# Attention's values in two products a key tile instead of three, with the weight sums taken by adding DMAs

## The chip, the cores and the metric

The kernel runs on one core of a Trainium2 chip. The metric is the device time of one execution in microseconds: the median over runs, 3317.97 us before the change (3 runs, 3317.39 to 3322.92 us). A difference under 0.2%, some 6.6 us, is about what such a measurement cannot tell from none.

## The reference

One layer of a bidirectional hybrid encoder on 2048 + 256 tokens of width 1024, all in float32: an RMS norm and one input projection, eight mLSTM heads (forward and backward) beside eight attention heads of dimension 64 (two key/value heads, q and k normed and rotated), an output projection, then a gated MLP with a width-3 convolution. The part that the change touches is the attention:

```python
s = jnp.einsum('bqhgd,bkhd->bhgqk', qi, k).astype(jnp.float32) * scale
p = jax.nn.softmax(s, axis=-1)
return jnp.einsum('bhgqk,bkhd->bqhgd', p.astype(v.dtype), v)
```

Each row of the softmax needs both the product of the exponentials with the values and the sum of the exponentials over all keys.

## The kernel before

The kernel has four stages on one timeline. Phase A (to about 220 us) norms and projects all tokens to q, k, v and the gates and stores them in DRAM. Then attention and mLSTM run mixed: two generators, `attention` and `mlstm`, are stepped in turn by `run_both` so that both finish at a set ratio, and when mLSTM is done, `phase_c` (the output projection, tile `po`, L1001) is stepped beside the rest of attention. Phase D (the MLP, from about 1760 us) ends the kernel. The calls only emit instructions; a scheduler of the framework then sets each engine's order by its own simulated clock and by priorities, and each engine runs its own list strictly in that order.

Float32 matrix products are made of rounded parts: a number is split in a high part (rounded to the type `F32R`, which TensorE takes in one pass) and a low part, the rest. A product of two such numbers is high x high + high x low + low x high.

Attention works on 36 half blocks (`hbs`): 512 query columns of one head (or of two heads for the 256 short tokens) against all their keys. 32 have 16 key tiles of 128, taken two at a time as 8 key pairs (`kp`); four have one key pair. That is 260 key pairs. For each:

- `scores` (L576 to L590): four products of 512 columns into the two-bank PSUM tile `ps` (L583, L584), ScalarE's exponential into `pe` (L587), ScalarE's rounding of it into the high part of `xx` (L588), VectorE's difference into the low part (L589). `pe` has PEB = 2 buffers, `xx` XB = 4.
- `values` (L592 to L602), which follows PLAG = 3 key pairs later: for each of the two key tiles three products of 512 columns into the accumulator `pv` (one bank, 128 rows). The weights tile `vv` holds the high part of v in its columns 0 to 63 and ones in columns 64 to 127, so rows 64 to 127 of `pv` collect the sums of the weights. `vl` holds the low part of v. The products are `vv` with high `xx` (L600), `vl` with high `xx` (L601), `vv` with low `xx` (L602).
- `maxstep` (L545): for the next half block, two products (`px`, L560) and one VectorE maximum (L562), so that the maxima are known before its first exponential.

When the last key pair's values are done, `fin1` (L604) copies the values to `o1` and the sums to `rs` with four ScalarE copies (L612); one key pair later `fin2` (L614) takes reciprocals, multiplies, and stores to `mix_d` (L624). PSUM tiles of `scores`, `maxstep`, `prep` and `prep2` share one ring of two, tag `sc`.

GpSimd's list in this stage holds mLSTM's small steps: loads of `dm` and their triangular masks (L824, L828), the products `kw` (L793), the square roots `mr` (L97, L98), memsets, and the stores of attention's outputs (L624). A DMA that GpSimd issues stands in the same list: GpSimd first waits for the DMA's operands and only then goes on.

Of the kernel before, what the change touches and what calls it, by code (L numbers as in the profile page):

```python
# [70 lines left out]
PB = 4  # L71
PEB = 2
XB = 4
PLAG = 3
ZT = 3
# [382 lines left out]
def attention(g, tc, s1, s2, pp):  # L458
# [12 lines left out]
    def load_kv(grp, k0, k1, after=None):  # L471
# [6 lines left out]
        for t0 in range(0, n, 4):  # L478
            m = min(4, n - t0)
            s = f"{n}_{t0}"  # L480
            kk = sp.tile([P, m * P], F32R, tag="kk" + s, name=f"kk{grp}_{s}", bufs=1)
            kl1 = sp.tile([65, m * P], F32R, tag="kl1" + s, name=f"kl1{grp}_{s}", bufs=1)
            vv = sp.tile([P, m, P], F32R, tag="vv" + s, name=f"vv{grp}_{s}", bufs=1)
            vl = sp.tile([P, m, HD], F32R, tag="vl" + s, name=f"vl{grp}_{s}", bufs=1)
            c = slice((k0 + t0) * P, (k0 + t0 + m) * P)
            if after is not None:
                for t in (kk[0:1, 0:1], kk[HD:HD + 1, 0:1], kl1[0:1, 0:1], vv[0:1, 0, 0:1], vl[0:1, 0, 0:1]):
                    nc.gpsimd.tensor_copy(t, after[0:1, 0:1])
            nc.gpsimd.memset(f32(vv[:, :, HD:P]), 1.0)
            for r in (0, HD):  # L490
                nc.gpsimd.dma_start(f32(kk[r:r + HD, :]), g.k_d[grp, 0:HD, c])
            nc.gpsimd.dma_start(f32(kl1[0:HD, :]), g.k_d[grp, HD:P, c])
            nc.gpsimd.memset(f32(kl1[64:65, :]), 1.0)
            for a, t in ((0, vv[:, :, 0:HD]), (1, vl)):
                nc.gpsimd.dma_start(f32(t), g.v_d[grp, :, k0 + t0:k0 + t0 + m, a])
            parts.append((kk, kl1, vv, vl))

# [79 lines left out]
    def scores(s, kp):  # L577
# [10 lines left out]
        nc.scalar.activation(x[:, 0], pe, AF.Copy)  # L588
        nc.vector.tensor_tensor(x[:, 1], pe, f32(x[:, 0]), ALU.subtract)  # L589
        return kp, x  # L590

    def values(s, kp, x):  # L592

        if kp == 0:
            s.pv = pp.tile([P, 512], F32, tag="pv", name="pv" + s.nm, bufs=1)
        vv, vl = s.kv[kp // 2][2:4]
        for z in range(2):
            kt = 2 * kp + z
            x1, x2 = (x[:, a, z * 512:(z + 1) * 512] for a in range(2))
            nc.tensor.matmul(s.pv, vv[:, kt % 4, :], x1, start=kt == 0, stop=False)  # L600
            nc.tensor.matmul(s.pv[0:HD], vl[:, kt % 4, :], x1, start=False, stop=False)  # L601
            nc.tensor.matmul(s.pv, vv[:, kt % 4, :], x2, start=False, stop=kt == s.nk - 1)  # L602

    def fin1(s):  # L604

        s.o1 = sp.tile([P, 256], F32, tag="o1", name="o1" + s.nm, bufs=1)
        if s.n == len(hbs) - 3:
            g.hold = s.o1
        s.rs = sp.tile([P, 256], F32, tag="rs", name="rs" + s.nm, bufs=1)
        for z in range(2):  # L610
            for r, o in ((0, s.o1), (HD, s.rs)):
                nc.scalar.activation(o[HD * z:HD * z + HD], s.pv[r:r + HD, 256 * z:256 * z + 256], AF.Copy)  # L612

    def fin2(s):  # L614
        for t in range(2):
# [23 lines left out]
    def drain():  # L639
        b, kp, x = pend.pop(0)  # L640
        values(b, kp, x)
        if kp == b.nk // 2 - 1:
            fin1(b)
            fins.append(b)

    for n in range(len(hbs)):
# [4 lines left out]
        for kp in range(nkp):  # L651
            pend.append((cur, *scores(cur, kp)))
            ready = bool(fins)
            if len(pend) > PLAG:
# [6 lines left out]
            if ready:  # L661
                fin2(fins.pop(0))
            yield 2.3
# [5 lines left out]
    while pend:  # L669
        drain()  # L670
        yield 1
    for b in fins:
        fin2(b)

# [777 lines left out]
def body(tc, aps, phases="abcd"):  # L1452
# [5 lines left out]
    with ExitStack() as st:  # L1458
# [35 lines left out]
        with ExitStack() as s2:  # L1494
# [26 lines left out]
            pm = pool(s_m, "m_p", bufs=MB, space=PSUM, side="right")  # L1521
            sk = pool(s2, "b_k", bufs=1)
            sa = pool(s2, "b_s", bufs=2)
            pa = pool(s2, "b_p", bufs=SCB, space=PSUM)
# [138 lines left out]
```

## Time and profile before

| what | value |
|---|---|
| median of the runs | 3317.97 us |
| span of the profiled execution | 3315.5 us (the runs' median is 2.5 us above it: what lies around the span) |
| TensorE (PE) busy | 3240.5 us, 98% |
| VectorE (DVE) busy | 2429.5 us, 73% |
| ScalarE (ACT) busy | 1993.5 us, 60% |
| GpSimd (POOL) busy | 522.1 us, 16% |
| bytes moved by DMA | 612.31 MB, 185 GB/s in the mean |
| first and last start of a score product (L583) | 219.7 and 1748.7 us |

Busy time of PE is a union of modelled intervals that overlap: a product of 512 columns is shown as some 400 ns long, but the next one starts before its end. What a product costs is read from the distance of two starts. A DMA row gives the kilobytes of one DMA and the median time from its issue to its landing.

### The profile page before, as it was taken

To read this page: it belongs to the slowest core of one execution; us is meant where nothing else is said; L and a number is where in the kernel's file an instruction comes from. 1 tells how busy PE (TensorE), PEld (TensorE's weight loads), DVE (VectorE), ACT (ScalarE), POOL (GpSimd) and SP (SyncE) were. 2 spreads that over 40 slices of the span, in tenths; PEclk is the share of its full clock that TensorE was granted. 3 is DMA by queue.
4 is the path that set the end of the run, shared out by engine and by line. 5 is a ranking of instruction groups with operands and counts; after the bars stand their busy time and mean duration, and the time that the engine had idled before them with its cause. 6 is when DMAs were issued, how large, how long until landed. Compare 5 with 4: busy or idle time off the path is not lost.

```text
span 3315.5 us, 53149 instructions
## 1 busy us (share of the span) xinstructions
PE 3240.5 (98%) x19488; PEld 3018.0 (91%) x19488; DVE 2429.5 (73%) x3759; ACT 1993.5 (60%) x3738; POOL 522.1 (16%) x917
## 2 busy tenths in 40 slices
PE   8989999999999999999999999999999999999998
PEld 7878888888888888788889999999999999999998
DVE  7755676676657768866666899998888889666654
ACT  5646666666675776655454555665676667454543
POOL 4561042223224323200000000000000000020101
PEclk9999999999999999999999999999999999999999
DMA  9973333343346444423227666767676567968663
GB/s 353 316 213 101 112 103 113 98 125 109 99 139 189 123 147 127 139 96 106 76 93 266 220 222 213 248 229 271 202 254 240 194 224 239 320 216 276 216 226 134
DMA packets 359117, 612.31 MB, mean 185 GB/s; under 512 B 31029, under 2 KB 215271, under 8 KB 358855
## 3 DMA queue, kind: packets, MB, share of 16 engines
q1 hardware_dynamic: 329431, 563.14, 50.5%
q0 software_dynamic: 11856, 33.96, 3.8%
q10 hardware_dynamic: 17568, 11.80, 1.1%
q8 instruction: 154, 2.52, 0.3%
q14 instruction: 108, 0.88, 0.1%
HBM read 444.85 MB, written 163.93 MB: 184 GB/s over the span
## 4 chain that ended last, share of the span: by engine, by line
PE 83%; issue 5%; DMA 4%; ACT 3%; DVE 3%; POOL 2%; SPq 1%; POOLq 0%; ACTq 0%; DVEq 0%
PE pa L1164 17%; PE pc L1164 8%; PE pf L1428 7%; PE po L1001 6%; PE pb L1164 4%; PE mj L720 4%; PE pj L238 4%; PE mv L730 4%; PE ph L1428 3%; PE ps L583 3%; PE pv L602 3%; PE pv L600 3%; PE ps L584 3%; PE pv L601 3%; PE px L560 3%
## 5 line engine op out<-in xcount | busy, mean ns | idle before, releaser
L589 DVE TENSOR_TENSOR xx<-pe,xx 128x1024 fp32r<-128x1024 f32 x260 | 319.0, 1227 | 171.4 <-ACT xx L588 169.9
L587 ACT ACTIVATE pe<-ps 128x1024 f32<-128x1024 f32 x260 | 266.1, 1024 | 231.8 <-PE ps L584 215.0
L562 DVE TENSOR_REDUCE mx<-px 128x1 f32<-128x1024 f32 x256 | 310.5, 1218 | 100.6 <-PE px L560 100.0
L588 ACT ACTIVATE xx<-pe 128x1024 fp32r<-128x1024 f32 x260 | 275.1, 1058 | 5.2 <-PE pv L602 0.2
L1381 POOL TENSOR_TENSOR sq<-sq,sq 128x384 f32<-128x384 f32 x38 | 48.5, 1277 | 1382.7 <-ACT sq L1377 1302.2
L1001 PEld LDWEIGHTS po<-cmx,wo 128*128 128x128 f32 x1728 | 229.9, 189 | 19.5 <-DVE cx L1008 1.1
L1001 PE MATMUL po<-cmx,wo 128*128 128x256 f32 x1728 | 238.7, 283 | 1.4 <-DVE cx L1008 1.0
L1168 ACT ACTIVATE u<-pa 128x386 f32<-128x386 f32 (+2 forms) x264 | 128.9, 489 | 173.9 <-PE pa L1164 168.7
L600 PE MATMUL pv<-xx,vv 128*128 128x512 f32 x520 | 212.4, 408 | 10.5 <-ACT rs L612 6.0
L583 PE MATMUL ps<-qq,kk 128*128 128x512 f32 x520 | 213.8, 411 | 8.2 <-ACT pe L587 3.9
L602 PE MATMUL pv<-xx,vv 128*128 128x512 f32 x520 | 211.0, 406 | 3.5 <-DVE xx L589 3.4
L584 PE MATMUL ps<-qm,kl 65*128 65x512 f32 x520 | 208.9, 402 | 0.0
L601 PE MATMUL pv<-xx,vl 128*64 128x512 f32 x520 | 207.3, 399 | 0.0
L720 PEld LDWEIGHTS mj<-mn,wm 128*128 128x128 f32 x1296 | 178.3, 193 | 18.3 <-ACT og L736 4.5
L720 PE MATMUL mj<-mn,wm 128*128 128x256 f32 x1296 | 189.6, 288 | 2.8 <-ACT og L736 2.8
L730 PE MATMUL mv<-wm,mn 128*128 128x256 f32 x1296 | 189.9, 286 | 1.3 <-ACT qb L726 1.3
L730 PEld LDWEIGHTS mv<-wm,mn 128*128 128x128 f32 x1296 | 176.1, 190 | 15.2 <-ACT qb L726 2.3
L238 PE MATMUL pj<-w_a,n1T 128*128 128x512 f32 (+1 forms) x864 | 167.8, 353 | 11.0 <-ACT w_a L105 7.1
L560 PE MATMUL px<-kk,qq 128*128 128x512 f32 x512 | 167.2, 408 | 2.4 <-ACT pe L587 2.4
L238 PEld LDWEIGHTS pj<-w_a,n1T 128*128 128x128 f32 x864 | 141.3, 192 | 30.6 <-ACT w_a L105 7.1
L1164 PE MATMUL pc<-nt,wb 128*128 128x386 f32 (+2 forms) x792 | 148.0, 341 | 0.0
L831 ACT ACTIVATE dm<-dm,tm 128x128 f32<-128x128 f32 x288 | 94.8, 392 | 86.0 <-POOL dm L828 85.7
(337 smaller groups left out, 8106.0 us busy)
## 6 DMA issues: line engine op xcount, KB each, us to landing
mn<-n_d SPq DMA_DIRECT2D x216, 256.0 KB, 3.1
ru<-w_up SPq DMA_DIRECT2D x88, 512.0 KB, 5.1
rs<-wsu_d SPq DMA_DIRECT2D x88, 512.0 KB, 5.7
act_d<-ts SPq DMA_DIRECT2D x33, 768.0 KB, 6.4
nt<-act_d SPq DMA_DIRECT2D x60, 384.0 KB, 5.2
re_t<-wsd_d SPq DMA_DIRECT2D x45, 512.0 KB, 5.4
wsu_d<-tw SPq DMA_DIRECT2D x44, 512.0 KB, 4.2
act_d<-ya SPq DMA_DIRECT2D x99, 192.0 KB, 2.1
```

Of the source, the lines that this page charges most:

```text
L238: nc.tensor.matmul(pjs[t][:, c0:c1], nTs[tiles[t]][:, c, a, :], ws[c][:, b, c0:c1], start=(c == 0 and k == 0), stop=(c == NCC - 1 and k == 2))
L562: nc.vector.tensor_reduce(s.mx[:, t0, z0:z0 + 1], ps, AX.X, ALU.max)
L583: nc.tensor.matmul(o, kk[:, kc:kc + P], s.qq, start=True, stop=False)
L584: nc.tensor.matmul(o, kl1[:, kc:kc + P], s.qm, start=False, stop=True)
L589: nc.vector.tensor_tensor(x[:, 1], pe, f32(x[:, 0]), ALU.subtract)
L600: nc.tensor.matmul(s.pv, vv[:, kt % 4, :], x1, start=kt == 0, stop=False)
L602: nc.tensor.matmul(s.pv, vv[:, kt % 4, :], x2, start=False, stop=kt == s.nk - 1)
L720: nc.tensor.matmul(pj[:, o].rearrange("p (n t) -> p n t", t=P), s.w[c][:, a, o * P:(o + 1) * P], nT[c][:, :, h, :], start=(c + o + k == 0) ...
L730: nc.tensor.matmul(pv[:, o], nT[c][:, o, a, :], s.w[c][:, h, 256:512], start=(c + o + k == 0), stop=(c == NCC - 1 and k == 2 and o == 1))
L1001: nc.tensor.matmul(po[:, o], wo[c][z // 2][:, a, n], mx[c][:, h, :], start=c + o + k == 0, stop=c == NCC - 1 and o == 1 and k == 2)
L1164: s.nc.tensor.matmul(p, w[:, aa, c, :], ops[k][:, c, bb, 0:s.n], start=c == 0 and i == 0 and not add, stop=c == NCC // 2 - 1 and i == 2, s ...
L1428: nc.tensor.matmul(ps[c], w[:, aa, c, :], t[:, gi - g0, bb, 0:H], start=gi == 0 and m == 0 and not more, stop=gi == NG - 1 and m == 2, ski ...
```

## The change

Each key tile gets two products instead of three: the weights tile `vv` now holds v's high part in columns 0 to 63 and its low part in columns 64 to 127, and the first product is that tile with the high part of `xx` (all 128 rows of `pv`), the second is v's high part alone with the low part of `xx` (rows 0 to 63). The ones are gone from the weights, so `pv` no longer holds the sums. Instead an adding DMA, issued by GpSimd, adds the previous key pair's `pe` (for the first, the pair before; a chain through the half block) into this key pair's `pe`, 128 x 1024 numbers in float32, 512 KB. After the last key pair GpSimd adds the two halves (`asum`), `fin2` splits it in high and low, and `fin3` multiplies both with a tile of ones on TensorE, which sums over the 128 partitions and spreads the result. `fin1` now adds the two halves of `pv`, and the old `fin2` is `fin4`. These four steps go out one key pair apart. PEB goes from 2 to 3, XB from 4 to 3, PLAG from 3 to 2.

```diff
-PEB = 2
-XB = 4
-PLAG = 3
+PEB = 3
+XB = 3
+PLAG = 2
...
         nc.vector.tensor_tensor(x[:, 1], pe, f32(x[:, 0]), ALU.subtract)
+        if kp:
+            nc.gpsimd.dma_start(pe, s.acc, accum_op=ALU.add)
+        s.acc = pe
+        if kp == s.nk // 2 - 1:
+            s.acc = sp.tile([P, 512], F32, tag="asum", name="asum" + s.nm, bufs=1)
+            nc.gpsimd.tensor_tensor(s.acc, pe[:, 0:512], pe[:, 512:1024], ALU.add)
...
-            nc.tensor.matmul(s.pv, vv[:, kt % 4, :], x1, start=kt == 0, stop=False)
-            nc.tensor.matmul(s.pv[0:HD], vl[:, kt % 4, :], x1, start=False, stop=False)
-            nc.tensor.matmul(s.pv, vv[:, kt % 4, :], x2, start=False, stop=kt == s.nk - 1)
+            for a in (0, 1) if z == 0 else (1, 0):
+                if a:
+                    nc.tensor.matmul(s.pv[0:HD], vv[:, kt % 4, 0], x2, start=False, stop=False)
+                else:
+                    nc.tensor.matmul(s.pv, vv[:, kt % 4].rearrange("p a d -> p (a d)"), x1, start=kt == 0,
+                                     stop=kt == s.nk - 1)
...
         for z in range(2):
-            for r, o in ((0, s.o1), (HD, s.rs)):
-                nc.scalar.activation(o[HD * z:HD * z + HD], s.pv[r:r + HD, 256 * z:256 * z + 256], AF.Copy)
+            r, c = slice(HD * z, HD * z + HD), slice(256 * z, 256 * z + 256)
+            nc.scalar.activation(o2[r], s.pv[HD:P, c], AF.Copy)
+            nc.vector.tensor_tensor(s.o1[r], s.pv[0:HD, c], o2[r], ALU.add)
+
+    def fin2(s):
+
+        s.ah = sp.tile([P, 2, 512], F32R, tag="ah", name="ah" + s.nm, bufs=1)
+        nc.scalar.activation(s.ah[:, 0], s.acc, AF.Copy)
+        nc.vector.tensor_tensor(s.ah[:, 1], s.acc, f32(s.ah[:, 0]), ALU.subtract)
+
+    def fin3(s):
+
+        ps = pp.tile([P, 1024], F32, tag="sc", name="pa" + s.nm)
+        for a in range(2):
+            nc.tensor.matmul(ps[:, 0:512], g.onesr, s.ah[:, a], start=a == 0, stop=a == 1)
+        s.rs = sp.tile([P, 256], F32, tag="rs", name="rs" + s.nm, bufs=1)
+        for z in range(2):
+            r, c = slice(HD * z, HD * z + HD), slice(256 * z, 256 * z + 256)
+            nc.scalar.activation(s.rs[r], ps[r, c], AF.Copy)
```

What moves on GpSimd's list, first before. The place is mLSTM's first head pair, token tiles 12 and 13 (`dm0_12`, `dm0_13` are its masks, `mr0_9` its square roots, `kw1_4` the next head pair's weighted keys):

```order
L824 DMA dm0_12_6657<-nm_d_71 128x512
L828 AFFINE_SELECT dm0_12_6657<-dm0_12_6657 128x256 x2
L97 TENSOR_SCALAR mr0_9_6525<-mms0_9_6522 128x2
L98 TENSOR_TENSOR mr0_9_6525<-mr0_9_6525,mhalf_80 128x2
L836 DMA ogr0_14_7072<-og_d_72 128x256
L737 MEMSET va1_3_4907 128x4
L793 TENSOR_TENSOR kw1_4_6427<-mkt1_2_6425,tm_91 128x256
L793 TENSOR_TENSOR kw1_5_6429<-mkt1_2_6425,tm_91 128x256
L824 DMA dm0_13_6928<-nm_d_71 128x512
```

The same place after the change; `pe0_4_5` is the exponentials of head 0, first query tile 4, key pair 5:

```order
L588 DMA pe0_4_5_4996<-pe0_4_4_4951 128x1024
L847 DMA dm0_12_6675<-nm_d_71 128x512
L851 AFFINE_SELECT dm0_12_6675<-dm0_12_6675 128x256 x2
L588 DMA pe0_4_6_5069<-pe0_4_5_4996 128x1024
L97 TENSOR_SCALAR mr0_9_6544<-mms0_9_6541 128x2
L98 TENSOR_TENSOR mr0_9_6544<-mr0_9_6544,mhalf_80 128x2
L588 DMA pe0_4_7_5126<-pe0_4_6_5069 128x1024
L859 DMA ogr0_14_7092<-og_d_72 128x256
L816 TENSOR_TENSOR kw1_4_6446<-mkt1_2_6444,tm_91 128x256
L816 TENSOR_TENSOR kw1_5_6448<-mkt1_2_6444,tm_91 128x256
L592 TENSOR_TENSOR asum0_4_5132<-pe0_4_7_5126 128x512
```

Every adding DMA now stands between mLSTM's steps, reads what the DMA before it wrote, and what follows it on the list cannot start before it has been issued.

On TensorE's list, late in attention, between the scores of key pairs 2 and 3 of head 7, first query tile 8 (`ps7_8_2`, `ps7_8_3`; `po` is phase C's product, `px` the next half block's maxima, `pv` the values), before:

```order
L1001 MATMUL po3_1_18752<-cmx3_3_18146,wo3_0_17023 128x256
L1001 MATMUL po3_1_18752<-cmx3_4_18150,wo4_0_17049 128x256 x3
L1001 MATMUL po3_1_18752<-cmx3_5_18154,wo5_0_17059 128x256 x2
L560 MATMUL px4_12_0_1_17648<-kk1_16_8_10489,qq4_12_17519 128x512
L560 MATMUL px4_12_0_1_17648<-kk1_16_12_10500,qq4_12_17519 128x512
L1001 MATMUL po3_1_18752<-cmx3_5_18154,wo5_0_17059 128x256
L1001 MATMUL po3_1_18752<-cmx3_6_18158,wo6_0_17105 128x256 x3
L1001 MATMUL po3_1_18752<-cmx3_7_18592,wo7_0_17115 128x256 x3
L145 MATMUL rs_c2_18708<-ident_73,rcol_c2_18711 128x128 x2
L1001 MATMUL po3_1_18752<-cmx3_0_18134,wo0_0_16977 128x256 x3
L1001 MATMUL po3_1_18752<-cmx3_1_18138,wo1_0_16987 128x256 x3
L583 MATMUL ps7_8_3_17717<-qq7_8_17076,kk1_16_4_10478 128x512
```

The same stretch after:

```order
L581 MATMUL ps7_8_2_17688<-qm7_8_17135,kl11_16_4_10505 128x512
L607 MATMUL pv7_8_17699<-xx7_8_0_17589,vv1_16_0_10498 128x512
L605 MATMUL pv7_8_17699<-xx7_8_0_17589,vv1_16_0_10498 64x512 x2
L607 MATMUL pv7_8_17699<-xx7_8_0_17589,vv1_16_0_10498 128x512
L607 MATMUL pv7_8_17699<-xx7_8_1_17636,vv1_16_0_10498 128x512
L557 MATMUL px4_12_0_1_17704<-kk1_16_8_10512,qq4_12_17578 128x512
L557 MATMUL px4_12_0_1_17704<-kk1_16_12_10520,qq4_12_17578 128x512
L580 MATMUL ps7_8_3_17776<-qq7_8_17133,kk1_16_4_10504 128x512
```

Here no product of phase C is left between the two key pairs. Counted over the whole list, mLSTM's projections end before key pair 170 of 260 after the change (before: around key pair 195), and the last 91 key pairs share TensorE with 1323 products of `po`. In blocks of 13 key pairs, from the 170th on, these are 257, 169, 179, 205, 0, 342 and 171.

30 lines of the change are left out of this document (15 added, 15 removed).

## The prediction

> **What bounds the kernel now.** I read the page's busy times first, then the table of stages, then who TensorE waits for, then the order of time. The busy times, and below them the table of stages (columns: stretch and its length, then busy time and instructions of PE, PEld, DVE, ACT and POOL, PE's clock, DMA share, GB/s):
>
> ```profile
> PE 3240.5 (98%) x19488; PEld 3018.0 (91%) x19488; DVE 2429.5 (73%) x3759; ACT 1993.5 (60%) x3738; POOL 522.1 (16%) x917
> ```
>
> ```profile
> 220.00:1400.00 1180.00, 1153.98 (x7283) 1004.43 (x7283) 809.37 (x1519) 771.11 (x1761) 334.46 (x657) 1.00 0.41 125
> 1400.00:1760.00 360.00, 352.88 (x2199) 306.10 (x2200) 239.28 (x333) 195.83 (x277) 14.69 (x23) 1.00 0.29 94
> ```
>
> Attention lies between 220 and 1760 us: first beside mLSTM, from about 1400 us beside phase C. In both PE is busy 98%, DVE 69% and 66%, ACT 65% and 54%. The same table for the exponentials alone (L587) counts the key pairs in each stage:
>
> ```profile
> 220.00:1400.00 1180.00, 200.60 (x196) 1.00 0.41 125
> 1400.00:1760.00 360.00, 65.47 (x64) 1.00 0.29 94
> ```
>
> So a key pair comes every 1540 / 260 = 5.9 us, in both stages. PE's waits from 220 to 1760 us, longest in total first (us, times, longest):
>
> ```profile
> PE pv L600 <- ACT rs L612: 6.0, 5, 1.9
> PE pv L600 <- ACT xx L588: 4.1, 6, 1.1
> PE ps L583 <- ACT pe L587: 3.9, 8, 1.6
> ```
>
> Even the longest total is 6 us of 1540. TensorE's own list sets the pace of this stage, and only what shortens that list shortens the kernel.
>
> **The products.** Their cost is the distance of two starts. Two stretches of PE in order of time:
>
> ```profile
> 929.05 0.40 PE L600 MATMUL pv<-xx,vv 128*128 128x512 f32 x1
> 929.28 0.39 PE L601 MATMUL pv<-xx,vl 128*64 128x512 f32 x1
> 929.51 0.40 PE L602 MATMUL pv<-xx,vv 128*128 128x512 f32 x1
> 929.75 0.40 PE L600 MATMUL pv<-xx,vv 128*128 128x512 f32 x1
> ```
>
> ```profile
> 1527.93 1.95 PE L1001 MATMUL po<-cmx,wo 128*128 128x256 f32 x15
> 1529.72 0.39 PE L602 MATMUL pv<-xx,vv 128*128 128x512 f32 x1
> ```
>
> A product of 512 columns takes 0.70 / 3 = 0.233 us, the one with 64 columns of weights (L601) as long as the others, so a narrower product saves nothing and a dropped one saves all of it. One of `po` takes 1.79 / 15 = 0.12 us. The counts are in the page:
>
> ```profile
> L600 PE MATMUL pv<-xx,vv 128*128 128x512 f32 x520 | 212.4, 408 | 10.5 <-ACT rs L612 6.0
> L602 PE MATMUL pv<-xx,vv 128*128 128x512 f32 x520 | 211.0, 406 | 3.5 <-DVE xx L589 3.4
> L601 PE MATMUL pv<-xx,vl 128*64 128x512 f32 x520 | 207.3, 399 | 0.0
> ```
>
> One of three groups goes: 520 x 0.233 = 121 us off PE. Two products with ones for each of 36 half blocks come in: 72 x 0.233 = 17 us. PE's list gets 104 us shorter. (The busy times would say 207 us; they overlap.)
>
> **The adding DMA.** Nothing in this trace adds by DMA, and nothing copies from on-chip memory to itself. The main queue's load (packets, MB, share of 16 engines) and the nearest rows (KB each, us from issue to landing):
>
> ```profile
> q1 hardware_dynamic: 329431, 563.14, 50.5%
> ...
> mn<-n_d SPq DMA_DIRECT2D x216, 256.0 KB, 3.1
> ...
> wsu_d<-tw SPq DMA_DIRECT2D x44, 512.0 KB, 4.2
> ...
> n_d<-n1T SPq DMA_DIRECT2D x18, 1024.0 KB, 8.0
> dm<-nm_d POOLq DMA_DIRECT2D x72, 256.0 KB, 3.7
> ...
> rd<-w_down SPq DMA_DIRECT2D x22, 512.0 KB, 3.3
> ```
>
> Below, 3.3 us: a plain 512 KB, the second read free. Above, 8.0 us: the row of 1024 KB. Between them I charge a second pass over 512 KB. The q1 row gives 563.14 MB in 50.5% of 3315.5 us, 336 GB/s with all 16 engines, so 524,288 bytes cost 1.6 us: 3.3 + 1.6 = 4.9 us on quiet engines, 4.2 + 1.6 = 5.8 us on busy ones. The DMA share here (0.41 and 0.29) lies between; GpSimd's queue adds 0.6 us at 256 KB (3.7 against 3.1), and a target on the chip instead of DRAM may take as much off, which no row shows. I take 5.3 us and keep both ends.
>
> The nearest plain row for 512 KB is 4.2 us. The Trainium skill has a fit for such a copy from GpSimd (DMA: Bandwidth & Descriptors, "Anatomy of one DMA — SWDGE (gpsimd) path"): about 2.0 us fixed plus the bytes at 436 GB/s, 3.2 us here; and it says of an add inside the DMA engine that its cost is the second source read on the same ring, which halves the rate (Collectives: The Full Stack, "The bandwidth ceiling: the fold count and why AG ≠ RS ≠ AR"). Together, as an estimate from these two pages, 2.0 + 2.4 = 4.4 us; by that the change would come out at about 3265 us, on the faster side.
>
> **The chain.** In a half block each add reads what the one before it wrote, so seven follow each other; then `asum` waits for the last, and the next half block's first add stands behind `asum` on GpSimd's list. With three `pe` buffers the exponential of key pair n + 3 waits until add n + 1 has read buffer n. So the adds set a second pace. `asum` is about the size of this one:
>
> ```profile
> L1381 POOL TENSOR_TENSOR sq<-sq,sq 128x384 f32<-128x384 f32 x38 | 48.5, 1277 | 1382.7 <-ACT sq L1377 1302.2
> ```
>
> With 1.3 us for it and 0.5 us to hand over, eight key pairs take 7 x 5.3 + 1.8 = 38.9 us, 4.86 us each. Where PE has more than that between two key pairs, the chain is hidden; where it has less, PE waits.
>
> Beside mLSTM PE has more. In the order after the change this stage holds 169 key pairs; its 196 before take 1180 us. Without 27 of them (some 2.8 us each, twelve products) and with 0.4 us less on each of the rest it is about 1180 - 76 - 68 = 1036 us, 6.1 us a key pair. The mean is covered; key pairs that stand close together are not. I allow 15 us (0 to 45).
>
> Beside phase C PE has less. Ten products of 512 columns a key pair are 2.33 us, and `po` adds to that by blocks of 13 key pairs, with the counts of the order: 257, 169, 179, 205, 0, 342 and 171 of 0.12 us. With each block's own products the blocks come to 4.7, 3.9, 4.1, 4.2, 2.5, 5.4 and 3.4 us a key pair (the last has hardly any `px`). Against 4.86 us the block without `po` loses 13 x 2.35 = 31 us, the last 19, the others 2, 13, 10, 9 and 0: 82 us together. A block with more work can't lend to its neighbour, since three buffers hold less than one block.
>
> **GpSimd's list.** Two of its waits (us, times, longest):
>
> ```profile
> POOL dm L828 <- DMA dm<-nm_d: 188.7, 66, 5.1
> POOL kw L793 <- PE mu L806: 169.5, 45, 21.1
> ```
>
> Each add waits for VectorE's difference and for the add before it, and behind it stand mLSTM's masks, `mr` and `kw`; VectorE and then PE wait for these. GpSimd waits much already, and mLSTM's steps run ahead of their use, so I take 10 us (0 to 40).
>
> **The rest.** The order of time shows one key pair on ACT and DVE:
>
> ```profile
> 902.70 1.03 ACT L587 ACTIVATE pe<-ps 128x1024 f32<-128x1024 f32 x1
> ...
> 904.08 1.06 ACT L588 ACTIVATE xx<-pe 128x1024 fp32r<-128x1024 f32 x1
> ...
> 905.17 1.23 DVE L589 TENSOR_TENSOR xx<-pe,xx 128x1024 fp32r<-128x1024 f32 x1 [1.31 <-ACT xx L588]
> ...
> 917.09 0.59 ACT L539 ACTIVATE qq<-pq 128x512 fp32r<-128x512 f32 x1
> ```
>
> From the exponential's start to the difference's end 3.7 us pass; values two key pairs later (some 9.7 us) still find `xx` ready, so PLAG 2 and XB 3 cost nothing while the pace holds. ACT's four copies a half block stay four; 0.59 us for `ah` comes in: 21 us in all. DVE gets two small adds and a difference of half the size above, about 1.4 us, 50 us in all. Over 1436 us DVE would be at (809 + 239 + 50) / 1436 = 76%, ACT at 69%: hidden under PE. The loads of `vl` and the memsets of ones go; they are off the path. At attention's end stand one more add, `asum`, `ah` and the product with ones before the last store; phase C's products cover part: 8 us.
>
> **The sum.** -121 + 17 + 82 + 15 + 10 + 8 = +11 us on a span of 3315.5 us, 3326.5 us; with the 2.5 us by which the median lies above it 3329 us.
>
> **The rivals.**
>
> 1. The chain keeps pace: an add takes 4.2 us, like the plain store of 512 KB. Then eight key pairs take 31.2 us, 3.9 each; only the block without `po` (13 x 1.4 = 18 us) and the last one (6) still lose, 25 us with a rest of 1; 5 us beside mLSTM, 5 on GpSimd, 6 at the end: -104 + 41 = -63 us, 3255 us. For it: the row itself, and a DMA share of 0.29 beside phase C. Against: a second stream must be read somewhere. It decides from about 5.1 us an add downwards, where the sum is zero. Chance 0.38. (The Trainium skill's 4.4 us, above, falls here too.)
> 2. The chain becomes the bound throughout: 6.3 us an add, from contention with mLSTM's loads. 5.74 us each: beside phase C the blocks lose 13, 25, 21, 20, 42, 4 and 30 us, 155; beside mLSTM 45, GpSimd 25, the end 10: -104 + 235 = +131 us, 3449 us. For it: 5.8 us above, and the 8.0 us row. At 8 us an add (7.2 us each) the whole stage would run at the chain's pace, some 400 us longer. Chance 0.22.
>
> My own case, 4.9 to 5.8 us an add, has 0.40 and reaches from 3295 us (blocks 58 us at 4.9 us an add) to 3390 us (117 us at 5.8). The range: 3245 us takes in rival 1, 3480 us rival 2 but not its far end. A measurement tells 0.2%, 6.6 us, from none. Faster: rival 1 and the lower end of my case, 0.44; within 0.2%: 0.08; slower: 0.48. The sign hangs on the add's time alone.
>
> **What would show it.** Right: products of `pv` fall to 1040; the adding DMAs land in 4.9 to 5.8 us; TensorE's list beside mLSTM stays 98% busy and waits beside phase C, behind exponentials that wait for a DMA; attention's last score starts about as late as before. Rival 1: adds near 4.2 us, PE at 95% or more to attention's end, the last score 60 us or more earlier. Rival 2: adds over 6 us, DMA waits of ACT beside mLSTM too. Wrong altogether: PE waits for GpSimd's `kw` or `mr`, or for DVE, while the adds are short.

## The result, and the profile after

| | before | after |
|---|---|---|
| median of the runs | 3317.68 us (3316.84 to 3322.92) | 3551.71 us (3549.93 to 3559.68) |
| ratio, 95% interval | | 1.0714 (1.0695 to 1.0734) |
| profiled span | 3315.5 us | 3557.8 us |
| mean granted clock of TensorE (1 is full speed) | 0.992 | 0.958 |
| last start of mLSTM's weight load for `mN` | 1387.3 us | 1451.5 us |
| last start of an exponential | 1749.4 us | 1990.6 us |

The change costs 234 us, 7.1%, and all of it lies in attention: the last exponential starts 241 us later, and what follows is as long as before. The forecast was 3329 us.

The busy times after, and the table of stages, cut where mLSTM ends (columns as before: stretch, its length, busy time and instructions of PE, PEld, DVE, ACT and POOL, PE's clock, DMA share, GB/s):

```profile
PE 3289.0 (92%) x19040; PEld 3012.6 (85%) x19040; DVE 2496.9 (70%) x3867; ACT 2016.5 (57%) x3774; POOL 745.5 (21%) x1154
```

```profile
220.00:1466.00 1246.00, 1103.37 (x6678) 941.83 (x6677) 797.35 (x1529) 731.68 (x1716) 470.98 (x799) 0.95 0.71 178
1466.00:2000.00 534.00, 457.69 (x2427) 371.22 (x2428) 323.39 (x438) 261.92 (x363) 100.45 (x119) 0.89 0.62 145
```

The same for the exponentials alone (L584):

```profile
220.00:1466.00 1246.00, 175.52 (x172) 0.95 0.71 178
1466.00:2000.00 534.00, 90.88 (x89) 0.89 0.62 145
```

Before, PE was 98% busy in both stages; now it is 89% and 86% busy. A key pair comes every 1246 / 172 = 7.2 us beside mLSTM (6.0 before) and every 534 / 89 = 6.0 us beside phase C (5.6 before), and 89 of the 260 come after mLSTM where 64 did. PE, its waits from 220 to 2000 us (us, times, longest):

```profile
PE ps L580 <- ACT pe L584: 47.0, 33, 4.1
PE px L557 <- ACT pe L584: 34.1, 25, 3.9
PE pv L607 <- ACT xx L585: 33.6, 25, 4.0
```

PE waits for ScalarE; before, the longest total of any wait was 6 us. Whom ScalarE and GpSimd wait for stands in the groups of the exponentials and of the adding DMAs (busy time, mean ns, then idle time ahead of them and what ended it):

```profile
L584 ACT ACTIVATE pe<-ps 128x1024 f32<-128x1024 f32 x260 | 266.4, 1025 | 393.5 <-DMA pe<-pe 264.6 <-PE ps L581 110.0 <-PE po L1024 6.2
L588 POOL DMA_DIRECT2D pe<-pe x224 | 199.5, 891 | 738.4 <-DMA pe<-pe 264.8 <-DVE xx L586 228.2 <-issue 39.2
```

The exponentials stand 264.6 us behind the landing of an add, GpSimd another 264.8. The adds themselves, as landings of the 224 and as load of their queue (packets, MB, share of 16 engines; before, this queue had 3.8%):

```profile
DMA to landing us min/median/max: 4.5/5.2/8.6
```

```profile
q0 software_dynamic: 43952, 151.42, 21.4%
...
pe<-pe POOLq DMA_DIRECT2D x224, 512.0 KB, 5.2
mn<-n_d SPq DMA_DIRECT2D x216, 256.0 KB, 4.1
```

An add lands in 5.2 us (the median; 5.55 in the mean of the 224), where 5.3 had been forecast. So the size on which "the sign hangs" was right, and the time was not. How the chain looks, in GpSimd's and ScalarE's order of time (start, length; in brackets the idle time ahead of it and what ended it):

```profile
1654.28 0.87 POOL L588 DMA_DIRECT2D pe<-pe  x1 [5.22 <-DMA pe<-pe]
1659.33 0.85 POOL L588 DMA_DIRECT2D pe<-pe  x1 [4.18 <-DMA pe<-pe]
1664.97 0.86 POOL L588 DMA_DIRECT2D pe<-pe  x1 [4.79 <-DMA pe<-pe]
1669.76 1.28 POOL L592 TENSOR_TENSOR asum<-pe 128x512 f32<-128x512 f32 x1 [3.94 <-DMA pe<-pe]
1676.33 0.87 POOL L588 DMA_DIRECT2D pe<-pe  x1 [5.29 <-DVE xx L586]
1683.59 0.85 POOL L588 DMA_DIRECT2D pe<-pe  x1 [6.39 <-DVE xx L586]
```

```profile
1658.88 1.03 ACT L584 ACTIVATE pe<-ps 128x1024 f32<-128x1024 f32 x1 [1.53 <-DMA pe<-pe]
...
1664.52 1.02 ACT L584 ACTIVATE pe<-ps 128x1024 f32<-128x1024 f32 x1 [2.04 <-DMA pe<-pe]
...
1671.08 0.63 ACT L624 ACTIVATE ah<-asum 128x512 fp32r<-128x512 f32 x1 [4.03 <-POOL asum L592]
...
1672.66 1.03 ACT L584 ACTIVATE pe<-ps 128x1024 f32<-128x1024 f32 x1
```

Three adds and `asum` follow each other at the pace of a landing (5.05, 5.64, 4.79 us). Then 6.57 us pass from `asum` to the next half block's first add, which waits for VectorE's difference: that key pair's exponential had itself started late, at 1672.66 us, behind ScalarE's copy for `ah`, which waits for `asum` and so for the last landing. In 14 of the 31 steps from one half block to the next this exponential (its second) starts within 0.1 us of the last landing, which the ring of three buffers makes it wait for; in 13 others the copy for `ah` stands between, and it starts up to 3.1 us behind the landing. Over the 32 half blocks of eight key pairs, worked out from the records of L584, L586 and L588: an add is issued 1.3 us in the mean after the one before it has landed (0.5 us where nothing else holds it), seven adds and six hand-overs take 46.6 us, 7.6 us pass to the next half block's first add, and a half block takes 54.5 us (mean over all 31 steps), 6.8 us a key pair. Forecast were 38.9 us and 4.86.

### The profile page after: what moved, and what is told of

Read it like the earlier page. It is cut to its first block, busy times and chain, and to the rows that moved or that the text cites. A ratio compares the mean times of both kernels' runs of the same rounds, so it can differ in the third digit from the quotient of the medians.

```text
span 3557.8 us, 52872 instructions
## 1 busy us (share of the span) xinstructions
PE 3289.0 (92%) x19040; PEld 3012.6 (85%) x19040; DVE 2496.9 (70%) x3867; ACT 2016.5 (57%) x3774; POOL 745.5 (21%) x1154
## 3 DMA queue, kind: packets, MB, share of 16 engines
q0 software_dynamic: 43952, 151.42, 21.4%
## 5 line engine op out<-in xcount | busy, mean ns | idle before, releaser
L584 ACT ACTIVATE pe<-ps 128x1024 f32<-128x1024 f32 x260 | 266.4, 1025 | 393.5 <-DMA pe<-pe 264.6
L586 DVE TENSOR_TENSOR xx<-pe,xx 128x1024 fp32r<-128x1024 f32 x260 | 321.8, 1238 | 233.4 <-ACT xx L585 232.3
L588 POOL DMA_DIRECT2D pe<-pe x224 | 199.5, 891 | 738.4 <-DMA pe<-pe 264.8
L580 PE MATMUL ps<-qq,kk 128*128 128x512 f32 x520 | 233.0, 448 | 60.8 <-ACT pe L584 47.0
L1024 PEld LDWEIGHTS po<-cmx,wo 128*128 128x128 f32 x1728 | 237.8, 197 | 29.8 <-ACT cmx L995 14.0
L607 PE MATMUL pv<-xx,vv 128*128 128x512 f32 x520 | 224.6, 442 | 34.5 <-ACT xx L585 33.6
L557 PE MATMUL px<-kk,qq 128*128 128x512 f32 x512 | 183.5, 442 | 50.3 <-ACT pe L584 34.1
L581 PE MATMUL ps<-qm,kl 65*128 65x512 f32 x520 | 222.2, 427 | 0.0
L743 PE MATMUL mj<-mn,wm 128*128 128x256 f32 x1296 | 198.8, 296 | 11.8 <-ACT og L759 5.6
L605 PE MATMUL pv<-xx,vv 128*64 128x512 f32 x520 | 181.4, 430 | 15.6 <-DVE xx L586 14.9
L580 PEld LDWEIGHTS ps<-qq,kk 128*128 128x128 f32 x520 | 107.7, 207 | 96.7 <-ACT pe L584 61.4
L607 PEld LDWEIGHTS pv<-xx,vv 128*128 128x128 f32 x520 | 106.6, 205 | 82.8 <-ACT xx L585 49.0
```

The costliest lines, as they stand in the source:

```text
L580: nc.tensor.matmul(o, kk[:, kc:kc + P], s.qq, start=True, stop=False)
L584: nc.scalar.activation(pe, ps, AF.Exp)
L607: nc.tensor.matmul(s.pv, vv[:, kt % 4].rearrange("p a d -> p (a d)"), x1, start=kt == 0, stop=kt == s.nk - 1)
L743: nc.tensor.matmul(pj[:, o].rearrange("p (n t) -> p n t", t=P), s.w[c][:, a, o * P:(o + 1) * P], nT[c][:, :, h, :], start=(c + o + k == 0) ...
L1024: nc.tensor.matmul(po[:, o], wo[c][z // 2][:, a, n], mx[c][:, h, :], start=c + o + k == 0, stop=c == NCC - 1 and o == 1 and k == 2)
```

## The experiments

The theory to be tried: the chain of adds sets the pace in both stages, through hand-overs (from one add's landing to the next one's issue) and block ends (from the last landing of a half block to the next one's first add), which the prediction had at next to nothing. Rivals: the ring of three `pe` buffers does it; the traffic does it; GpSimd's list does it; or the rest of the change would not have brought its 104 us even without adds. Times are medians, ratios stand against runs of the kernel before on the same chip, which lay between 3313.5 and 3318.5 us.

**Without the adds.** The adding DMA left out of the changed kernel. The sums then cover the last key pair alone, and 1e-6 is added to them so that they stay above zero (here and in all runs below that leave sums out or change them):

```diff
-        if kp:
-            nc.gpsimd.dma_start(pe, s.acc, accum_op=ALU.add)
         s.acc = pe
```

> The changed kernel without the adding DMAs (the sums cover the last key pair only, with 1e-6 added so that they stay above zero). If the adds and the waits for them are the whole loss: the product saving alone, 3318 - 104 + 10 for attention's end = about 3225 us (3205 to 3250). If the smaller buffers (XB 3, PLAG 2), the new steps at a half block's end or the new order cost as well: over 3260 us.

3311.45 us, ratio 0.9984 (0.9975 to 0.9994). Even with no add at all the change is worth 6 us and not 104. That alone takes 98 us of what the prediction had counted on.

**Without the chain.** The same bytes into the same buffer, but the source is the key pair's own low part, so that no add reads what another wrote (the sums then hold other numbers):

```diff
-            nc.gpsimd.dma_start(pe, s.acc, accum_op=ALU.add)
+            nc.gpsimd.dma_start(pe, f32(x[:, 1]), accum_op=ALU.add)
```

> The same adding DMAs, as many, as large, at the same places of GpSimd's list, but each adds its own key pair's low part of xx to pe instead of the previous pe, so no add waits for another and none reads another's result (the sums are wrong by that). Chain theory (add after add, each waiting for the last one's landing): 3230 to 3290 us. Traffic or list theory (the bytes slow the other loads, or the adds on GpSimd's list hold up mLSTM's small steps): 3400 us or more, since both stay.

3434.45 us, ratio 1.0353 (1.0335 to 1.0371). By the bounds set ahead this is the theory of traffic or list, but both have a part: the chain is worth 3552 - 3434 = 117 us, and adds without a chain still cost 3434 - 3311 = 123 us.

**A fourth buffer.** The room for it is taken from `asum` and `o2`, which share the tile `ah` here, and from `o1`, which has one buffer instead of two (only the first line of the edit is shown):

```diff
-PEB = 3
+PEB = 4
```

> The changed kernel with four pe buffers instead of three (to make room asum and o2 live in ah, rounded, and o1 has one buffer). Ring theory (the exponential waits for an add's landing, and at a half block's start exponential, rounding and difference of 3.4 us stand between the last landing and the next first add): the 7.6 us from one chain to the next fall to about 3 us, 32 x 4.6 = 147 us less, about 3405 us. Pure chain theory (seven adds of 6.8 us in series): within 40 us of 3552 us.

3538.86 us, ratio 1.0667 (1.0649 to 1.0685), 13 us less. The wait moves with it: the exponentials wait 67.8 us for landings instead of 246.9 (220 to 1950 us), and GpSimd 299.4 instead of 242.2. Some 20 of the 31 second exponentials of a half block now start before the last landing, and yet the block end takes 6.6 us where it took 7.6. The ring is where much of the chain was felt, and little of what made it slow.

**The sums on GpSimd.** A GpSimd instruction takes the place of the DMA:

```diff
-            nc.gpsimd.dma_start(pe, s.acc, accum_op=ALU.add)
+            nc.gpsimd.tensor_tensor(pe, pe, s.acc, ALU.add)
```

> GpSimd itself adds (128 x 1024, some 3.4 us each by the 1277 ns of 128 x 384) instead of issuing an adding DMA; chain and ring as before. Chain theory: 3.4 us stand in for 5.5 us landing and 1.3 us hand-over, eight key pairs take 7 x 3.6 + 5 = 30 us, less than TensorE's 43: 3225 to 3290 us. List theory: 224 x 3.4 = 760 us of GpSimd stand in front of mLSTM's masks, kw and mr: 3400 us or more, with PE waiting beside mLSTM and not beside phase C.

3445.03 us, ratio 1.0386 (1.0371 to 1.0402). It gains 107 us over the changed kernel, with no landings and no transfers, and still stands 134 us above the run without adds. GpSimd's sum, and VectorE's difference beside it:

```profile
L588 POOL TENSOR_TENSOR pe<-pe,pe x224: 2344/2397/3847, 269.3 to 1878.0; 128x1024 f32<-128x1024 f32 x112
```

```profile
L586 DVE TENSOR_TENSOR xx<-pe,xx 128x1024 fp32r<-128x1024 f32 x260 | 372.0, 1431 | 113.9 <-ACT xx L585 113.1
```

The sum takes 2.40 us and the difference 1.43 instead of 1.24; 260 of them are 50 us of VectorE, and TensorE now waits for the low part of `xx` (45.2 us, where it is 21.4 without adds). The differences are the smaller part of what VectorE loses: it is busy 2705.6 us, 215 more than without adds, with as many instructions. mLSTM's update of `C` takes 0.64 us instead of 0.32.

**Two products alone.** To see where the 104 us went, the kernel before with one line removed, the product of v's low part (so that part of v is left out; ones, sums, rings and lists stay):

```diff
-            nc.tensor.matmul(s.pv[0:HD], vl[:, kt % 4, :], x1, start=False, stop=False)
```

> The kernel before with one edit: the product of v's low part is left out, so each key tile has two products; ones, sums, ring sizes, steps and GpSimd's list stay as they were. It stands for the prediction's first term alone. TensorE's list sets the pace: 520 products x 0.233 us come off, 3317 - 121 = 3196 us (3185 to 3215). Rival, that the shorter list uncovers the waits of the exponential and the difference behind it, as the run without adds (3311) would have it: 3240 us or more, TensorE idle near 150 us of the span where it was 75, and in TensorE's list 184 key pairs ahead of mLSTM's last product where the kernel before has 193.

3251.54 us, ratio 0.9805 (0.9791 to 0.9820): 64 us come off, not 121. With the changed kernel's sizes as well (`PEB = 3`, `XB = 3`, `PLAG = 2`):

> As the run before this one (one product of three left out, nothing else), and with it the changed kernel's sizes: three buffers of the weights before rounding in place of two, three of the rounded in place of four, values two key pairs late in place of three. The prediction had these sizes at nothing: within 10 us of the run before. If they are what ate the gain of the run without adds: 50 to 100 us longer than the run before, near 3290 to 3310, with TensorE waiting for the difference.

3248.48 us, ratio 0.9797 (0.9782 to 0.9812): the sizes cost nothing here, as the prediction had it. The same sizes in the whole kernel before:

> The kernel before, whole, with the changed kernel's three sizes alone (three buffers before rounding, three rounded, values two key pairs late). With three products TensorE has 2.8 us of its own a key pair and the prediction sees no cost: 3310 to 3328 us. If the sizes cost by themselves: 3340 us or more.

3332.06 us, ratio 1.0048 (1.0033 to 1.0063), 17 us more, a little outside its bounds: with three products the sizes are felt, with two they aren't. Which of the three it is was not tried. The stages of the run with two products and the new sizes, and its exponentials (L587):

```profile
220.00:1320.00 1100.00, 1056.96 (x6799) 941.56 (x6798) 783.50 (x1495) 750.14 (x1733) 338.23 (x653) 0.99 0.45 134
1320.00:1700.00 380.00, 363.93 (x2263) 317.75 (x2261) 265.14 (x368) 220.50 (x314) 17.18 (x28) 0.99 0.29 93
```

```profile
220.00:1320.00 1100.00, 190.37 (x186) 0.99 0.45 134
1320.00:1700.00 380.00, 75.45 (x74) 0.99 0.29 93
```

PE stands still for 43 + 16 = 59 us of these 1480, where it was 26 + 7 = 33 of 1540 before, and its clock is 0.99 and not 1.00, another 15 us (an estimate, 0.01 x 1480). With 0.5 us less to do a key pair, TensorE meets waits that it used to come to late. That is about 41 of the 54 us that this run lacks of the 121; where the rest goes is open.

**The ones.** The run without adds, less `ah` and the two products with ones a half block (the copies to `rs` read `asum`):

```diff
-        ps = pp.tile([P, 1024], F32, tag="sc", name="pa" + s.nm)
-        for a in range(2):
-            nc.tensor.matmul(ps[:, 0:512], g.onesr, s.ah[:, a], start=a == 0, stop=a == 1)
...
-            nc.scalar.activation(s.rs[r], ps[r, c], AF.Copy, bias=1e-6)
+            nc.scalar.activation(s.rs[r], s.acc[r, c], AF.Copy, bias=1e-6)
```

> The run without adds, less the spreading of the sums: no rounded sums ah, no products with ones, no turn in the ring of two PSUM tiles that scores share; the copies to rs read asum itself (so the sums lack key tiles and are not spread). By the prediction this leaves out 17 us of products, 3311 - 17 = 3294 us. If the turn that these products take in the ring, and what it moves in the list, is what stands between 3311 and the 3248 of two products with the old sums: 3250 us (3235 to 3265); in TensorE's list 188 key pairs then stand ahead of mLSTM's last product, where the run without adds has 173.

3263.65 us, ratio 0.9829 (0.9808 to 0.9850): 48 us less than with them. And with them, but `ah` made by GpSimd instead of ScalarE and VectorE:

> No adds (3311), and the rounded sums ah made by GpSimd as in the run before this one, while the products with ones keep their turn in the ring of two PSUM tiles (the sums lack key tiles, as without adds). Without these products and ah it was 3264. If ScalarE's and VectorE's steps for ah are the 48 us between: 3265 to 3280 us. If the products' turn in the ring and in TensorE's list are: 3300 to 3315 us.

3316.52 us, ratio 1.0002 (0.9991 to 1.0013): the steps for `ah` on ScalarE and VectorE are not it, which leaves the products. 72 products of 0.233 us are 17 us; the other 31 must come with their place. The tile `pa` takes a turn in the ring of two that scores and maxima share, and the schedule changes with it. The number of key pairs whose scores stand ahead of mLSTM's last product into `mN` in TensorE's list:

| | key pairs ahead of it | time, us |
|---|---|---|
| before | 193 | 3317.7 |
| two products, new sizes | 186 | 3248.5 |
| without adds, without the ones | 188 | 3263.7 |
| without adds | 173 | 3311.5 |
| changed kernel | 170 | 3551.7 |

Without adds, the products with ones push 15 key pairs behind mLSTM, where TensorE has less to do between them. The count alone does not give the time: with `ah` made by GpSimd it is 177, and the time is 3316.5 us. The stages and exponentials of the run without adds:

```profile
220.00:1320.00 1100.00, 1048.13 (x6729) 918.20 (x6728) 806.63 (x1544) 743.79 (x1731) 359.02 (x654) 0.99 0.44 133
1320.00:1760.00 440.00, 404.94 (x2360) 337.38 (x2359) 308.89 (x427) 251.48 (x349) 31.82 (x40) 0.95 0.26 82
```

```profile
220.00:1320.00 1100.00, 180.00 (x176) 0.99 0.44 133
1320.00:1760.00 440.00, 85.92 (x84) 0.95 0.26 82
```

84 key pairs at 5.24 us after mLSTM, where the run with two products and the new sizes has 74 at 5.14; PE is 92% busy there at a clock of 0.95. Whether the turn in the ring or the order alone does it was not told apart.

**What adds cost beside their chain.** A GpSimd sum of one column, then of 384 columns, at the place of each add: the same waits in GpSimd's list, and no transfer.

```diff
-            nc.gpsimd.dma_start(pe, s.acc, accum_op=ALU.add)
+            nc.gpsimd.tensor_tensor(pe[:, 0:1], pe[:, 0:1], s.acc[:, 0:1], ALU.add)
```

> The changed kernel with a GpSimd sum of one column (128 x 1) at the place of each adding DMA: the same waits for the difference and for the one before it stand in GpSimd's list, but there is no transfer, no landing and next to no time on the port (the sums lack all other columns; a small number is added to them). If the 123 us that adds without a chain cost (3434 against 3311 without adds) are mLSTM's small steps standing in GpSimd's list behind the wait for the difference: 3400 us or more. If they are the transfers and the buffers that these hold: 3311 us (3300 to 3330), like the run without adds.

> The changed kernel with a GpSimd sum of 384 columns at the place of each adding DMA (the sums lack the others): by the 2.4 us of 1024 columns it takes about 1.0 us, as long as GpSimd spends issuing an adding DMA, and there is no transfer and no landing. If GpSimd's time in its list is the cost: 3400 to 3430 us, like adds without a chain. If the transfer and its landing are: 3340 to 3360 us, a little above the sum of one column (3336).

3335.56 us, ratio 1.0050 (1.0030 to 1.0070), and 3337.82 us, ratio 1.0064 (1.0040 to 1.0088). GpSimd's list costs 24 us, and its time in it next to nothing: as the cause of the 123 us, the theory of the list falls. Smaller adds, in the same chain (512 columns, then 128):

```diff
-            nc.gpsimd.dma_start(pe, s.acc, accum_op=ALU.add)
+            nc.gpsimd.dma_start(pe[:, 0:512], s.acc[:, 0:512], accum_op=ALU.add)
```

> The changed kernel with adding DMAs of the first 512 columns alone, 256 KB in place of 512 (the sums lack the odd key tiles; a small number is added to them so that the reciprocal is finite); as many DMAs, in the same chain. If an add's time goes with its size, it lands in about 2.8 us, a half block takes 7 x (2.8 + 1.3) + 7.5 = 36 us, 4.5 a key pair, and the chain is hidden beside mLSTM: 3340 us (3310 to 3380), little above the run without adds. If most of an add is fixed, it lands in 4 us or more, a half block takes 45 us, 5.6 a key pair: 3430 us or more.

> The changed kernel with adding DMAs of the first 128 columns alone, 64 KB in place of 512, as many and in the same chain (the sums lack the other columns; a small number is added to them). 256 KB landed in 3.7 us and 512 KB in 5.2, a fixed 2.2 us and 3.0 for 512 KB; so 64 KB should land in about 2.6 us, which a pace of 5.5 to 6 us a key pair hides with ease, and DMA traffic is that of the run without adds. If what a DMA costs beside the chain (3434 without a chain, 3432 at half the bytes, 3336 with a sum of one column) is the 0.88 us that GpSimd spends issuing each: 3410 to 3430 us. If it is the bytes, or the landing that is waited for: 3340 to 3370 us.

3431.56 us, ratio 1.0340 (1.0320 to 1.0361), with 256 KB, and 3374.58 us, ratio 1.0173 (1.0146 to 1.0201), with 64 KB. Their landings:

```profile
DMA to landing us min/median/max: 3.2/3.7/7.8
```

```profile
DMA to landing us min/median/max: 2.1/2.7/5.9
```

The 2.7 us are as worked out (2.6): 2.2 us fixed and 3.0 us for 512 KB. The times forecast from the bytes were too low. Half the bytes bring 120 us and not 210: the exponentials still wait 106.8 us for landings, and the time is that of the whole adds without a chain. The run with 64 KB lies 5 us above what the theory of bytes and landings allowed and 35 below the least that the theory of GpSimd's issue asked for; so the cost beside the chain goes with the transfers, but not all of it with their bytes.

**The last add, and who waits for it.** ScalarE's copy for `ah` waits for `asum`, which waits for the last landing, so exponentials stand behind it. The run without a chain with `ah` on GpSimd, and the changed kernel with the same:

```diff
+            s.ah = sp.tile([P, 2, 512], F32R, tag="ah", name="ah" + s.nm, bufs=1)
+            nc.gpsimd.tensor_tensor(s.ah[:, 0], pe[:, 0:512], pe[:, 512:1024], ALU.add)
+            nc.gpsimd.tensor_tensor(s.ah[:, 1], s.acc, f32(s.ah[:, 0]), ALU.subtract)
```

> Adds without a chain (3434), and the rounded sums ah made by GpSimd, right behind asum in its list, in place of a ScalarE copy and a VectorE difference: neither engine's list holds a step that waits for the last add to land. In the run without a chain ScalarE stands 59 us behind asum for ah and VectorE 36 us behind that, with the next half block's exponentials queued behind; a GpSimd step of a microsecond costs next to nothing (3338 with 384 columns). If this boundary is what adds cost beside their chain: 3340 to 3370 us. If it is the transfers themselves (buffers held, mLSTM's loads at 4.6 us in place of 3.4): 3410 us or more.

> The changed kernel, whole, with ah made by GpSimd. The chain of seven adds stays (seven landings of 5.2 to 5.5 us and six hand-overs of 1.3, 46.6 us), and GpSimd has two more steps of 1.3 us between the last add of a half block and the next one's first: if the chain of transfers alone sets the pace, 3552 us or up to 36 x 2.6 = 94 us more. If ScalarE and VectorE waiting for the last add are a good part of what the chain costs: 3450 to 3500 us.

3432.01 us, ratio 1.0342 (1.0325 to 1.0359), and 3570.64 us, ratio 1.0768 (1.0742 to 1.0794). No gain without the chain, so there the theory falls. With the chain it is 19 us more, but this settles less: ScalarE's wait is gone, and GpSimd's two steps stand in the chain instead, so that the block end is 7.9 us.

**The adding itself.** The run without a chain less its last add a half block, so that `asum` waits for no landing; then the same with plain copies from SyncE (the edit shown); then plain copies from GpSimd:

```diff
-        if kp:
-            nc.gpsimd.dma_start(pe, f32(x[:, 1]), accum_op=ALU.add)
+        if 0 < kp < s.nk // 2 - 1:
+            nc.sync.dma_start(pe, f32(x[:, 1]))
```

> Adds without a chain (3434), less the last one of each half block: 192 adds, as large and at the same places; the sum asum reads a tile that no transfer writes, so nothing in GpSimd's list waits for a landing (there asum waits 117 us, with mLSTM's steps mr, dm and kw behind it). If that wait is what adds cost beside their chain: 3340 to 3370 us. If it is the adds' issue or their transfers: a seventh less than 98 above the sum of one column, 3410 to 3425 us.

> The run before this one with its 192 transfers as plain copies issued by SyncE: the same 512 KB from one tile in the core's own memory into the same buffer, which is held as long, but GpSimd issues none and mLSTM's loads of dm and ogr have GpSimd's queue for themselves (4.6 us for dm with adds, 3.7 without). If the transfers as such (traffic, buffers held) are the cost: within 20 us of the run before. If it is that they go through GpSimd's list and queue: 3330 us or less. A mishap that would blur it: mLSTM's loads mn stand behind these copies in SyncE's list, which would show as TensorE waiting for mn.

> The run of 192 adds without a chain and without the last one (3413), with plain copies in place of the adds, still issued by GpSimd. From SyncE the same copies cost next to nothing (3332) and landed in 3.5 us, where the adds landed in 5.6. If the cost is the way through GpSimd (0.87 us of issue, its queue shared with dm and ogr): 3400 us or more, with dm landing in 4.6 us or later. If it is the adding (a transfer that reads its destination as well holds the DMA engines longer): 3330 to 3350 us, with the copies landing near 3.5 us.

3412.95 us, ratio 1.0294 (1.0276 to 1.0313); 3331.59 us, ratio 1.0059 (1.0043 to 1.0076); 3345.55 us, ratio 1.0100 (1.0073 to 1.0128). The same 100 MB at the same places cost 81 us less as copies from SyncE, and 67 of these come off with copies from GpSimd, by the adding alone. An add also takes GpSimd 0.33 us longer to issue, but that can't be it: the sum of 384 columns takes 0.82 us more each than that of one column and costs a few us in all. Queue and issues of the run with adds:

```profile
q0 software_dynamic: 39344, 134.64, 19.7%
...
pe<-xx POOLq DMA_DIRECT2D x192, 512.0 KB, 5.6
mn<-n_d SPq DMA_DIRECT2D x216, 256.0 KB, 4.2
...
dm<-nm_d POOLq DMA_DIRECT2D x72, 256.0 KB, 5.1
```

Of the run with GpSimd's copies:

```profile
q0 software_dynamic: 39344, 134.64, 11.5%
...
pe<-xx POOLq DMA_DIRECT2D x192, 512.0 KB, 3.6
mn<-n_d SPq DMA_DIRECT2D x216, 256.0 KB, 3.8
...
dm<-nm_d POOLq DMA_DIRECT2D x72, 256.0 KB, 4.2
```

The bytes are equal; the share of the 16 engines is not. With SyncE's copies this queue has 3.7% left for all else. So the adds hold the engines as long as all 16 for (0.197 - 0.037) x 3401.4 / 192 = 2.8 us each and the copies (0.115 - 0.037) x 3344.1 / 192 = 1.4 us. The Trainium skill says of an add inside the DMA engine that the second source's read on the same ring halves the rate (Collectives: The Full Stack, "The bandwidth ceiling: the fold count and why AG ≠ RS ≠ AR"); the two shares agree with that.

Where it is lost: mLSTM's last weight load for `mN` starts at 1378.4 us with adds and 1337.2 us with copies, so 41 of the 57 us between the two spans are lost beside mLSTM. There `dm` lands 0.9 us later, and ScalarE waits 135 us for GpSimd's mask of it instead of 103, VectorE 67 us for `mr` instead of 51 (220 to 1330 us). That these waits are the way in which the adds reach TensorE is not shown, and one comparison speaks against it: the adds without a chain and the sum of one column, 99 us apart, have nearly the same two waits (98 and 63 us; 102 and 63). That an add's longer hold on the DMA engines is what costs the time is likewise argued from the shares; what a run shows is that adds cost 67 us more than copies.

## Why the prediction was wrong

The sum was -121 + 17 + 82 + 15 + 10 + 8 = +11 us. By the runs:

| term | forecast, us | measured, us | from |
|---|---|---|---|
| one product of three goes | -121 | -64 | two products alone, 3251.5 against 3315.4 |
| ring and lag sizes | 0 | -3 | two products, new sizes, 3248.5 |
| the other new steps (copies, `asum`, order of the products) | 0 | +15 | without adds and ones, 3263.7 |
| products with ones, and `ah` | +17 | +48 | without adds, 3311.5 |
| GpSimd's list | +10 | +24 | sum of one column, 3335.6 |
| the adds' transfers, without their chain | 0 | +99 | adds without a chain, 3434.5 |
| chain, bunching, attention's end | +82 +15 +8 = +105 | +117 | the change, 3551.7 |

The terms of the two columns add up to +11 and +236; the medians of different batches differ by a few us. (The losses of the seven blocks beside phase C add up to 84 us as the prediction prints them, and not 82, which changes nothing.)

- **"What bounds the kernel now" was read rightly, and too much was concluded.** TensorE's list did set the pace. But "only what shortens that list shortens the kernel" was taken to mean that it shortens the kernel by as much. A row that says PE waits 6 us tells what is late now, not what stands close behind it: with the product gone, 54 to 57 of its 121 us did not come off, and about 41 of them show as TensorE standing still and as its clock.
- **The products with ones were costed as PE time alone.** The prediction named no cover for their PSUM turn and took the schedule after the change (it counted 169 key pairs beside mLSTM) as given, without asking what put 27 fewer there. That they cost 48 us, with `ah`, where they are placed is shown; how much of it the ring makes and how much the order isn't.
- **The adding DMA's landing was right** (5.3 against 5.2 us), and the lower estimate beside it, 4.4 us, lies under the shortest of the 224 landings (4.5 us). The size of the chain in all came out near, 105 against 117 us, but by luck: its pace and its place were wrong. "Beside mLSTM PE has more. ... The mean is covered" failed: without the chain mLSTM's last `mN` load starts 55 us earlier and the stage behind it is 78 us shorter (461 against 539 us from there to the last exponential), the whole of the 133 us between the two spans. The hand-overs (1.3 us in the mean, forecast 0) and the block end (7.6 us, forecast 1.8) make 6.8 us a key pair of the forecast's 4.86. Over the forecast, the mean landing of 5.55 us adds 1.7 us a half block, the hand-overs 7.8, the block end 5.8. The block end was worked out as `asum` and a hand-over alone; in the trace the next half block's second exponential waits for the last landing too, through the ring or behind the copy for `ah`, and with it the difference for which the next add waits. The ring is not the whole of it: with a fourth buffer the block end still takes 6.6 us.
- **What a transfer takes from others was left out.** The sum priced an add where it is waited for, with its landing. It had no term for what the transfers cost mLSTM, whose loads share the DMA engines with them and landed later (`mn` 4.2 us with 192 adds, 3.8 with copies, 3.4 with neither). This is the largest single miss, 99 us. That the adding makes most of it is shown (67 us between adds and copies); by which wait it reaches TensorE is open. The prediction's second rival had "contention with mLSTM's loads", but as what makes the adds long, not what the adds make long.
- **The rivals.** "The chain becomes the bound throughout" is the nearest in time, 3449 us. One of its signs came true, exponentials that wait for landings beside mLSTM too (143 us from 220 to 1330 us); the other, adds over 6 us, did not. That its time lies nearest is in part luck: it had the chain at 155 + 45 + 10 = 210 us, which cost 117, and the product, the ones and the transfers as low as the forecast had them. The signs given for the likeliest case were wrong in two points: PE beside mLSTM is 89% busy, not 98, and the last score starts 232 us later (1980.9 against 1748.7).
- **What came true:** the new sizes cost nothing with two products.

No run with the whole computation is faster than the kernel before. The two runs with two products are 2% faster and leave v's low part out; they show what one product fewer a key tile brings.

## What to carry to other kernels

A row that says that the busiest engine waits for nothing tells the most that work taken off it can bring; it does not say that all of it comes off the time (here 64 us of 121 did). Run the removal alone first. A DMA in a chain costs its landing, its hand-over and the block end. Beside that its transfer costs something even where nothing waits for it, so price both; here an adding DMA held the engines twice as long as a copy, and 192 of them cost 67 us more. A new product that takes a turn in a shared PSUM ring can cost more than its own length (here 48 us for 17, `ah` included).

## What was not expected of the hardware

- A plain 512 KB copy inside the core's memory landed in 3.5 to 3.6 us (medians) whether SyncE or GpSimd issued it; the adding one took 5.2 in the chain and 5.6 to 5.7 without it, 4.5 at the least. GpSimd spent 0.56 us issuing a copy and 0.89 us issuing an add.
- The size law of the adds was near straight: 2.7, 3.7 and 5.2 us for 64, 256 and 512 KB.
- With GpSimd summing tiles of 128 x 1024 in 2.40 us each, VectorE's difference of that size took 1.43 us in the mean instead of 1.24 and its update of `C` 0.64 instead of 0.32; VectorE's busy time rose by 215 us in all.
- TensorE's granted clock was lower in the stages in which it waited more: 1.00 in both stages before (98% busy), 0.95 and 0.89 after (89% and 86%). In the run without adds it was 0.95 behind mLSTM (92%) at a DMA share of 0.26, so no adding transfers are needed for it. The longer busy time after the change (3289 us for 448 products fewer) goes with the lower clock.
